# Attention in a hybrid encoder: the product with the values moves behind the transposes of the next unit, into the free columns of one of its PSUM banks

## The chip, the cores and the metric

One core of a Trainium2 chip runs the whole kernel as one program. The metric is the device time of that program in microseconds, as the median of several executions; less is better. One execution was also recorded by the hardware profiler, and all rows below come from that one.

## What is computed

The reference is an encoder of two layers. Each layer normalizes its input, multiplies it by one wide projection, and runs three token mixers beside each other: windowed attention, an mLSTM and a Mamba-2 SSD. Their outputs go through output projections, are gated, summed and projected once more. Two sequences (256 and 512 tokens, together six tiles of 128) share the weights. Only attention is touched. Cut to that part (`...` marks what is left out):

```python
def window_attention(q, k, v, sink):
    ...
    s = jnp.einsum('bnqhgd,bnkhd->bnhgqk', qb, kw).astype(jnp.float32) * (ATT_HEAD_DIM ** -0.5)
    ...
    mx = jnp.maximum(jnp.max(s, axis=-1, keepdims=True), sk)
    p = jnp.exp(s - mx)
    p = p / (jnp.sum(p, axis=-1, keepdims=True) + jnp.exp(sk - mx))
    o = jnp.einsum('bnhgqk,bnkhd->bnqhgd', p.astype(v.dtype), vw)
    return o.reshape(bsz, s_len, ATT_HEADS * ATT_HEAD_DIM)
...
    ya = window_attention(aq, ak, av, attn_sink) * jax.nn.silu(az)
```

There are 8 query heads of width 64 and 2 heads of keys and values. A tile of 128 queries sees its own tile of keys and its neighbours in the same sequence, so two or three tiles.

## The kernel before

**The stream of large matmuls.** The program walks through a list of items (`ORDER`), each a projection from the normalized tokens or an output projection. A float32 number is split into a high and a low part of type float32r, and a product is three matmuls of such parts. These matmuls, 512 or 256 columns wide, are most of TensorE's work. `mm_c` and `mm_t` issue them and call `tick()` after every few.

**The mixers as filling.** The mixers are Python generators. `tick()` lets them issue as many steps as a planner (`Clock`) holds ready: it adds up a cost for every instruction on every engine, and a step may go when its inputs and its PSUM banks are free by the planner's time, which is that of TensorE (`now`). A generator says what it waits for: `yield` (its last step is done), `yield 1`, `yield 2` or `yield "pair"` (so many of the four PSUM banks 4 to 7, which `grab` gives out and `give` takes back), or a tuple (a flag that another step sets with `flag`). The order in which instructions are issued is so fixed when the program is built; on the chip semaphores, put in by the framework, hold an instruction until what it needs is there. The engines work through their queues in order.

**Attention.** `mix_att(l, g)` handles one group of four query heads in one layer. Its work is twelve units, one for each tile of queries and pair of heads, numbered here 0 to 11; a `Flow` keeps up to four of them in progress, each at least one step behind the one ahead. There are two layers and two groups, so four times twelve units, 48 in all. A unit's steps are:

1. Scores: two banks, one for each head; masked maximum on VectorE into the SBUF buffers `ps[0]` and `ps[1]`, 256 or 384 wide (`n`).
2. Exponentials with their sums on ScalarE, the reciprocal on VectorE, and the scaling by it on ScalarE (head 0) and GpSimd (head 1).
3. Transposes: two banks; TensorE transposes `ps[0]` into the first and `ps[1]` into the second, 128 columns at a time, and ScalarE copies each bank back into `ps[0]` and `ps[1]`.
4. Values: one more bank; TensorE multiplies the values by the transposed probabilities, head 0 into partitions 0 to 63 and head 1 into 64 to 127, 128 columns wide; VectorE multiplies the result by the gate.
5. ScalarE and GpSimd split that product into its high and low part.

In the profile the transposes of a unit are 4 MATMULs of 128 columns with two tiles of keys and 6 with three, one for each tile and head. The product with the values has 64 stationary columns (`128*64` in the rows); each of its float32 matmuls shows as two MATMULs, so it has 8 or 12.

**What hangs on attention.** In each layer the two groups run one after the other (`A0`, `A1`), then the four mLSTM heads, then the SSD. The item `oa0` in the large stream needs attention's output; `item_O` calls `finish_mixer((l, "A1"))` before it issues its first matmul, and this issues all that is left of attention at once.

The profile shows all instructions on line 332, which is the helper that records them for the planner; names (`psum<-F`, `psum<-H,R`) and shapes tell them apart. `H` holds the normalized tokens, `R` float32r data and split weights, `F` float32 data. MATMULs on `H,R` and `R,H`, and those on `R` 512 wide, are the large stream; those on `R` 256 or 384 wide in blocks of four are attention's scores.

Of the kernel before, what the change touches and what calls it, by code (L numbers as in the profile page):

```python
# [12 lines left out]
ALU = mybir.AluOpType  # L13
# [18 lines left out]
NT = 6  # L32
# [385 lines left out]
class Body:  # L418
# [1163 lines left out]
    def mix_att(self, l, g):  # L1582
        s, nc, F = self.S[l], self.nc, self.F
        v, sc = nc.vector, nc.scalar
        cb = s["cb"]
        yield Room(self.R, 4 * TOK)
        s["ya", g] = self.R.alloc(4 * TOK)
        if g == 0:
            yield Room(F, *[384] * 8, *[128] * 4, *[12] * 4)
            s["pr"] = Ring(F, 8, 384)  # L1590
            s["ar"] = Ring(F, 4, 128)
            s["as"] = Ring(F, 4, 12)
        q4 = s["q", g].ap.rearrange("p (h t) -> p h t", h=4)
        k4 = s["k"].ap.rearrange("p (x v t) -> p x v t", x=2, v=2)
        vv = s["v"].ap.rearrange("p (i c) -> p i c", i=NT)

        def unit(i, hp):
            seq = SEQ_TILES[0] if i < 2 else SEQ_TILES[1]
            ks = [j for j in (i - 1, i, i + 1) if j in seq]
            n = 128 * len(ks)  # L1600
            m0 = K_ATT + 128 * (ks[0] - i + 1)
            h0 = 4 * g + 2 * hp
            ts = slice(128 * i, 128 * i + 128)
            bs = yield 2
            sm = s["as"].next()
            ps = [s["pr"].next()[:, 0:n] for _ in range(2)]
            for e, b in enumerate(bs):
                for x in range(2):
                    nc.tensor.matmul(out=b[:, 0:n], lhsT=q4[:, 2 * hp + e, ts],
                                     rhs=k4[:, x, g, 128 * ks[0]:128 * ks[0] + n], start=x == 0, stop=x == 1)  # L1610
            for e, b in enumerate(bs):
                v.tensor_tensor_reduce(out=ps[e], in0=b[:, 0:n], in1=self.K[:, m0:m0 + n], scale=1.0, scalar=-3.0e38,
                                       op0=ALU.add, op1=ALU.max, accum_out=sm[:, e:e + 1])
            self.give(*bs)
            r, sink = s["qn"].ap[:, 8 * i + h0:8 * i + h0 + 2], cb[:, CB_SINK + h0:CB_SINK + h0 + 2]
            v.tensor_tensor(out=sm[:, 0:2], in0=sm[:, 0:2], in1=r, op=ALU.mult)
            v.scalar_tensor_tensor(out=sm[:, 2:4], in0=sm[:, 0:2], scalar=-1.0, in1=sink, op0=ALU.mult, op1=ALU.min)
            v.tensor_tensor(out=sm[:, 6:8], in0=sm[:, 2:4], in1=sink, op=ALU.subtract)
            yield
            for e in range(2):  # L1620
                sc.activation(out=ps[e], in_=ps[e], func=AF.Exp, bias=sm[:, 2 + e:3 + e], scale=r[:, e:e + 1],
                              accum_out=sm[:, 4 + e:5 + e])
            sc.activation(out=sm[:, 6:8], in_=sm[:, 6:8], func=AF.Exp)
            yield
            v.tensor_tensor(out=sm[:, 8:10], in0=sm[:, 4:6], in1=sm[:, 6:8], op=ALU.add)
            v.reciprocal(out=sm[:, 10:12], in_=sm[:, 8:10])
            yield
            sc.activation(out=ps[0], in_=ps[0], func=AF.Copy, scale=sm[:, 10:11])
            nc.gpsimd.tensor_scalar(out=ps[1], in0=ps[1], scalar1=sm[:, 11:12], scalar2=None, op0=ALU.mult)
            bs = yield 2  # L1630
            for e, b in enumerate(bs):
                for j in range(len(ks)):
                    self.transpose_to(b[:, 128 * j:128 * j + 128], ps[e][:, 128 * j:128 * j + 128])
            for e, b in enumerate(bs):
                sc.copy(ps[e], b[:, 0:n])
            self.give(*bs)
            b, = yield 1
            for j, kt in enumerate(ks):
                for e in range(2):
                    nc.tensor.matmul(out=b[64 * e:64 * e + 64, 0:128], lhsT=vv[:, kt, 64 * g:64 * g + 64],  # L1640
                                     rhs=ps[e][:, 128 * j:128 * j + 128], start=j == 0, stop=j == len(ks) - 1)
            o = s["ar"].next()
            v.scalar_tensor_tensor(out=o, in0=b[:, 0:128], scalar=0.5, in1=s["az", 2 * g + hp].ap[:, ts], op0=ALU.mult, op1=ALU.mult)
            self.give(b)
            yield
            y4 = s["ya", g].ap.rearrange("p (x j t) -> p x j t", x=2, j=2)
            hi, lo = (y4[:, x, hp, ts] for x in range(2))
            sc.copy(hi, o)
            yield
            nc.gpsimd.tensor_tensor(out=lo, in0=o, in1=hi.bitcast(F32), op=ALU.subtract)  # L1650

        yield Flow([unit(i, hp) for i in range(NT) for hp in range(2)], 4)
        s.pop(("q", g)).free()
        for j in (2 * g, 2 * g + 1):
            s.pop(("az", j)).free()
        if g == 1:
            for k in ("pr", "ar", "as", "k", "v", "qn"):
                s.pop(k).free()
# [336 lines left out]
```

## Time and profile before

| what | value |
|---|---|
| median of the runs timed | 1682.69 us (3 runs, 1682.54 to 1683.93) |
| the profiled execution | 1680.04 us |
| its span, first to last instruction | 1678.2 us |
| TensorE busy in the span | 1666.3 us, 99% |
| VectorE, ScalarE, GpSimd busy | 53%, 38%, 17% |
| granted clock of TensorE | 1.00 |

The profiled execution is 1.84 us longer than its span, which is what lies around the span. It is 2.65 us shorter than the median of the timed runs. A busy share of TensorE says that some matmul was in its pipeline; how densely the matmuls follow each other is read from their start times.

### The profile page before, as it was taken

How to read it: one execution, taken by the hardware profiler on the slowest of the kernel's cores; microseconds unless marked ns; L12 is line 12 of the kernel's file. 1: busy time of each engine (PE TensorE's matmuls, PEld its weight loads, DVE VectorE, ACT ScalarE, POOL GpSimd, SP SyncE). 2: the span in 40 equal slices, each digit the busy share in tenths (PEclk: the TensorE clock that was granted, in tenths of full speed). 3: DMA queues.
4: the chain of work that ended last, by engine and by line, in shares of the span. 5: the costliest groups of instructions: out<-in, count | busy, mean ns of one | idle time of the engine just before them, and what ended most of it. 6: DMA issues, size and time to landing. Idle time of an engine off the chain costs nothing. (4 is left out here: it accounts for less than half of the span.)

```text
span 1678.2 us, 25327 instructions
## 1 busy us (share of the span) xinstructions
PE 1666.3 (99%) x9898; PEld 1433.0 (85%) x9898; DVE 890.6 (53%) x2114; ACT 633.6 (38%) x1365; POOL 284.9 (17%) x398
## 2 busy tenths in 40 slices
PE   8999999999999999999999999999999999999999
PEld 6888888988887888888878878898888888888887
DVE  6663537644486962246347535465455869523541
ACT  5456653422333522233233646532332345132320
POOL 5513220000002020013034223100000020201220
PEclk9999999999999999999999999999999999999999
DMA  5110122222124633145202101222221146331522
GB/s 192 64 40 27 56 81 92 69 70 68 63 63 124 166 87 107 62 155 170 88 32 72 45 26 63 82 83 79 70 73 60 63 126 173 79 110 44 176 88 76
DMA packets 45434, 145.36 MB, mean 87 GB/s; under 512 B 5345, under 2 KB 6273, under 8 KB 45314
## 3 DMA queue, kind: packets, MB, share of 16 engines
q1 hardware_dynamic: 43010, 137.44, 24.6%
q0 software_dynamic: 2304, 6.29, 2.4%
q8 instruction: 78, 1.28, 0.3%
q14 instruction: 42, 0.34, 0.1%
HBM read 124.69 MB, written 19.02 MB: 86 GB/s over the span
## 5 line engine op out<-in xcount | busy, mean ns | idle before, releaser
L332 PE MATMUL psum<-H,R 128*128 128x512 f32 x4800 | 885.9, 340 | 0.0
L332 PEld LDWEIGHTS psum<-H,R 128*128 128x128 f32 x4800 | 734.1, 188 | 103.3 <-issue 5.1
L332 PE MATMUL psum<-R,H 128*128 128x512 f32 (+2 forms) x1752 | 386.5, 376 | 3.1 <-DVE H L332 1.6
L332 PEld LDWEIGHTS psum<-R,H 128*128 128x128 f32 x1752 | 305.0, 188 | 59.2 <-DVE H L332 2.5
L332 DVE TENSOR_TENSOR R<-F,R 128x1024 fp32r<-128x1024 f32 (+3 forms) x178 | 222.1, 1258 | 246.1 <-ACT R L332 244.5
L332 ACT ACTIVATE F<-F 128x128 f32<-128x128 f32 (+8 forms) x432 | 210.6, 517 | 184.6 <-DVE F L332 177.5
L332 DVE SCALAR_TENSOR_TENSOR F<-F 128x128 f32<-128x128 f32 (+5 forms) x644 | 236.4, 412 | 57.1 <-POOL F L332 31.3
L332 PE MATMUL psum<-F 128*128 128x128 f32 (+6 forms) x2002 | 251.4, 288 | 5.5 <-DMA F<-ng_dram 2.7
L332 PE MATMUL psum<-R 128*128 128x512 f32 (+2 forms) x1344 | 249.8, 336 | 0.0
L332 PEld LDWEIGHTS psum<-F 128*128 128x128 f32 (+3 forms) x2002 | 203.2, 162 | 48.0 <-issue 20.4
L332 ACT CAST R<-F 128x1024 fp32r<-128x1024 f32 (+3 forms) x226 | 194.6, 875 | 120.4 <-PE psum L332 52.4
L332 PEld LDWEIGHTS psum<-R 128*128 128x128 f32 x1344 | 203.9, 188 | 31.3 <-issue 4.6
L332 ACT ACTIVATE F<-psum 128x768 f32<-128x768 f32 (+2 forms) x124 | 89.2, 719 | 324.0 <-PE psum L332 313.4
L332 POOL TENSOR_TENSOR F<-F 128x512 f32<-128x512 f32 (+9 forms) x200 | 166.2, 841 | 253.3 <-ACT F L332 119.6
L332 POOL TENSOR_SCALAR F<-F 128x256 f32<-128x256 f32 (+9 forms) x114 | 81.5, 718 | 742.8 <-ACT F L332 524.2
L332 ACT COPY F<-psum 128x256 f32<-128x256 f32 (+6 forms) x262 | 95.5, 399 | 200.3 <-PE psum L332 193.1
L332 DVE SCALAR_TENSOR_TENSOR F<-F,psum 128x768 f32<-128x768 f32 (+3 forms) x124 | 88.5, 725 | 95.6 <-PE psum L332 53.0
L332 DVE SCALAR_TENSOR_TENSOR F<-psum,F 128x128 f32<-128x128 f32 (+4 forms) x75 | 37.5, 505 | 186.8 <-PE psum L332 182.8
L332 DVE TENSOR_TENSOR F<-F 128x2 f32<-128x2 f32 (+7 forms) x292 | 74.7, 266 | 26.0 <-ACT F L332 18.6
L332 DVE TENSOR_SCALAR F<-F 128x128 f32<-128x128 f32 (+3 forms) x206 | 59.4, 327 | 42.1 <-ACT F L332 22.2
L332 DVE TENSOR_TENSOR F<-F,psum 128x129 f32<-128x129 f32 (+2 forms) x104 | 35.8, 377 | 37.9 <-ACT F L332 23.0
L332 DVE CUSTOM_DVE_ANT_0 F<-psum,F 128x256 f32<-128x256 f32 (+1 forms) x96 | 40.9, 464 | 13.4 <-PE psum L332 13.1
(25 smaller groups left out, 277.1 us busy)
## 6 DMA issues: line engine op xcount, KB each, us to landing
F<-wts_dram SPq DMA_DIRECT2D x164, 512.0 KB, 3.6
F<-csd SPq DMA_DIRECT2D x32, 384.0 KB, 6.1
F<-x_dram SPq DMA_DIRECT2D x12, 512.0 KB, 6.2
F<-md SPq DMA_DIRECT2D x16, 384.0 KB, 5.6
mg<-F SPq DMA_DIRECT2D x16, 384.0 KB, 2.6
mg<-F POOLq DMA_DIRECT2D x16, 384.0 KB, 4.8
F<-mg SPq DMA_DIRECT2D x16, 384.0 KB, 4.2
x<-F SPq DMA_DIRECT2D x6, 512.0 KB, 2.6
```

Of the source, the lines that this page charges most:

```text
L332: r = fn(*args, **kw)
```

## The change

A unit no longer takes a bank of its own for the product with the values. After its transposes it leaves a function (`values`) in a list. The next unit of the same group, right after it has issued its own transposes and their two copies, calls that function with columns 384 to 511 of its first bank, which transposes use at most up to column 383. So the product of unit `num - 1` is issued behind the transposes of unit `num`, in the same step. Two flags order the steps: `"pr"` says that a unit's transposed probabilities are there, and the next unit issues no transposes before it; `"pv"` says that a unit's product has been issued, and its last two steps wait for it. The last unit of a group still takes a bank of its own.

```diff
+            o = s["ar"].next()
+
+            def values(b):
+                for j, kt in enumerate(ks):
+                    for e in range(2):
+                        nc.tensor.matmul(out=b[64 * e:64 * e + 64, :], lhsT=vv[:, kt, 64 * g:64 * g + 64],
+                                         rhs=ps[e][:, 128 * j:128 * j + 128], start=j == 0, stop=j == len(ks) - 1)
+                v.scalar_tensor_tensor(out=o, in0=b, scalar=0.5, in1=s["az", 2 * g + hp].ap[:, ts], op0=ALU.mult, op1=ALU.mult)
+
+            yield (l, "pr", g, num - 1) if num else None
             bs = yield 2
             for e, b in enumerate(bs):
                 for j in range(len(ks)):
                     self.transpose_to(b[:, 128 * j:128 * j + 128], ps[e][:, 128 * j:128 * j + 128])
             for e, b in enumerate(bs):
                 sc.copy(ps[e], b[:, 0:n])
+            self.flag(l, "pr", g, num)
+            if left:
+                left.pop()(bs[0][:, 384:512])
+                self.flag(l, "pv", g, num - 1)
             self.give(*bs)
-            b, = yield 1
-            for j, kt in enumerate(ks):
-                for e in range(2):
-                    nc.tensor.matmul(out=b[64 * e:64 * e + 64, 0:128], lhsT=vv[:, kt, 64 * g:64 * g + 64],
-                                     rhs=ps[e][:, 128 * j:128 * j + 128], start=j == 0, stop=j == len(ks) - 1)
-            o = s["ar"].next()
-            v.scalar_tensor_tensor(out=o, in0=b[:, 0:128], scalar=0.5, in1=s["az", 2 * g + hp].ap[:, ts], op0=ALU.mult, op1=ALU.mult)
-            self.give(b)
-            yield
+            if num < last:
+                left.append(values)
+                yield (l, "pv", g, num)
+            else:
+                b, = yield 1
+                values(b[:, 0:128])
+                self.give(b)
+                yield
```

Here `num = 2 * i + hp`, `last = 11`, and `left` is one list for the twelve units of a group.

## Rows read from the trace of the kernel before

**Rows 1.** The page: span, busy time and share of each engine.
```profile
span 1678.2 us, 25327 instructions
PE 1666.3 (99%) x9898; PEld 1433.0 (85%) x9898; DVE 890.6 (53%) x2114; ACT 633.6 (38%) x1365; POOL 284.9 (17%) x398
```

**Rows 2.** Waits of TensorE over the span: total us, times, longest; two largest of six.
```profile
PE psum L332 <- DMA F<-ng_dram: 2.7, 1, 2.7
PE psum L332 <- DVE H L332: 1.6, 2, 1.2
```

**Rows 3.** One stretch of attention: us, busy time by engine, PEclk, DMA share, GB/s.
```profile
113.00:184.00 71.00, 71.00 (x466) 57.69 (x465) 29.00 (x132) 44.80 (x138) 22.53 (x31) 1.00 0.07 23
```

**Rows 4.** Timeline of TensorE: start, us from start to last end, operation.
```profile
166.08 0.60 PE L332 MATMUL psum<-F 128*128 128x128 f32 x4
166.43 1.64 PE L332 MATMUL psum<-R,H 128*128 128x512 f32 x6
168.00 0.66 PE L332 MATMUL psum<-F 128*64 128x128 f32 x8
168.59 3.02 PE L332 MATMUL psum<-R,H 128*128 128x512 f32 x12
...
174.26 1.55 PE L332 MATMUL psum<-R,H 128*128 128x512 f32 x6
175.65 0.64 PE L332 MATMUL psum<-R 128*128 128x256 f32 x4
...
179.44 1.25 PE L332 MATMUL psum<-F 128*64 128x128 f32 x12
180.44 1.64 PE L332 MATMUL psum<-R,H 128*128 128x512 f32 x6
...
182.60 1.66 PE L332 MATMUL psum<-R,H 128*128 128x512 f32 x6
184.10 0.60 PE L332 MATMUL psum<-F 128*128 128x128 f32 x4
```

**Rows 5.** Timeline of all engines, 238.9 to 241.6 us (idle time before in brackets).
```profile
238.96 1.19 PE L332 MATMUL psum<-F 128*128 128x128 f32 x12
239.44 0.65 ACT L332 COPY F<-psum 128x256 f32<-128x256 f32 x2 [0.49 <-PE psum L332]
239.49 0.42 PEld L332 LDWEIGHTS psum<-F 128*64 128x64 f32 x8 [0.17 <-issue]
240.08 0.97 PE L332 MATMUL psum<-H,R 128*128 128x512 f32 x4
...
240.98 0.66 PE L332 MATMUL psum<-F 128*64 128x128 f32 x8
...
241.57 0.96 PE L332 MATMUL psum<-H,R 128*128 128x512 f32 x4
```

**Rows 6.** Timeline of TensorE and ScalarE, a unit with three tiles of keys.
```profile
151.49 0.82 PE L332 MATMUL psum<-F 128*128 128x128 f32 x6
...
152.07 0.86 ACT L332 COPY F<-psum 128x384 f32<-128x384 f32 x2 [1.02 <-PE psum L332]
```

**Rows 7.** Groups by shape, ScalarE, 113 to 242 us: busy us, mean ns.
```profile
L332 ACT COPY F<-psum 128x256 f32<-128x256 f32 x44 | 14.2, 376 | 18.8 <-PE psum L332 18.6
L332 ACT COPY F<-psum 128x384 f32<-128x384 f32 x16 | 6.9, 483 | 13.5 <-PE psum L332 11.3 <-issue 2.2
```

**Rows 8.** The chain that ended last, in order of time: start, us, what.
```profile
978.79 0.04 issue
978.84 460.68 PE psum L332 x2887
```

**Rows 9.** Groups by shape, TensorE, 241.6 to 249.95 us, then 1073.4 to 1084.05 us.
```profile
L332 PE MATMUL psum<-H,R 128*128 128x512 f32 x24 | 8.5, 398 | 0.0
...
L332 PE MATMUL psum<-H,R 128*128 128x512 f32 x24 | 8.8, 406 | 0.0
```

**Rows 10.** Timeline of TensorE behind the last product of attention, second layer.
```profile
1069.08 6.16 PE L332 MATMUL psum<-H,R 128*128 128x512 f32 x34
```

More of the change, by code (lines that the diff above doesn't have):

```diff
@@ L1595, in mix_att @@
         vv = s["v"].ap.rearrange("p (i c) -> p i c", i=NT)
+        left = []
+        last = 2 * NT - 1
         def unit(i, hp):
+            num = 2 * i + hp
             seq = SEQ_TILES[0] if i < 2 else SEQ_TILES[1]
```

## The prediction

> **What bounds the kernel now.** I read the page first: TensorE is busy in 1666.3 of 1678.2 us and no other engine is above 53% [rows 1]. The view of waits then says how little TensorE stands still: six rows, 8.2 us in all, 2.7 of it the first load and the rest mostly between the layers [rows 2]. In attention's stretch it never stands still, and its clock is 1.00, the 2.4 GHz level [rows 3]. So the end is set by what TensorE issues, one instruction behind the other, and whatever holds it back holds back the large stream queued behind. Work taken from ScalarE, VectorE or the banks is worth nothing unless it shortens TensorE's queue. A busy share of 99% hides losses between matmuls, so everything below is read from starts in the timeline.
>
> **What an insertion costs today.** In the rows, T is a unit's block of transposes, V its product with the values. Six matmuls of the stream alone take 1.39 us (174.26 to 175.65). Between a T and a V they take 1.57 (166.43 to 168.00), so leaving a T and entering a V cost 0.18 together; behind a V and ahead of a T they take 1.50 (182.60 to 184.10), so leaving a V costs 0.11 [rows 4]. T itself lasts 0.35 to the next start with four transposes (166.08 to 166.43), V 0.59 with eight matmuls (168.00 to 168.59) [rows 4]. A T and a V apart therefore cost 0.35 + 0.59 + 0.18 + 0.11 = 1.23 us.
>
> **What the move saves.** The change joins T of unit n with V of unit n-1, T first, 11 times in each of four runs of attention, 44 times. The trace has this order once already, on separate banks: T at 238.96, the first weights of V at 239.49, the stream again at 240.08 [rows 5]. That is 1.12 us, and 0.11 for leaving V makes 1.23: the same as apart. T takes 0.53 ahead of a V where it takes 0.35 ahead of the stream, so the cost of turning from 128 to 64 stationary columns is paid either way. The other order, V first and T behind it, is cheaper: 1.00 for the two (179.44 to 180.44), plus the 0.18, is 1.18 [rows 4]. Going through the list of blocks, I counted this order at 21 of the 48 products of before, seven with matmuls 512 wide alone in front and fourteen with pairs of 512 and 256. After the change a T that directly follows a V is unlikely, since it must wait for the copies of the T before. So the move loses 21 x 0.05 = 1.05 us and saves nothing. No instruction is added or removed on TensorE, and no DMA is touched; ScalarE, VectorE and GpSimd do what they did.
>
> **What the move adds.** Both blocks now use one bank. ScalarE's copy of `bs[0]` is issued before V and reads that bank; V writes other columns of it. I take it that the framework orders accesses to PSUM bank by bank, so that the first weight load of V waits for this copy (not for the copy of `bs[1]`, which is another bank). No row of before has such a pair, since every product had a bank of its own; the kernel's own code points the same way, for the last columns of the last tile take a fresh pair of banks (`if c0 == 768: p = self.gbank()[:, 256:512]`) where the bank just being read had room. From below the price is nothing, if columns are told apart. From above it is the time until the second copy ends. Between them I take the first copy, as the code issues it.
>
> The price with two tiles of keys: T starts at 238.96, ScalarE begins the first copy at 239.44 [rows 5], a copy takes 0.376 [rows 7], so it ends at 239.82; TensorE starts 0.05 after the instruction that it waited for (978.79 to 978.84) [rows 8], so at 239.87. Without the wait it started at 239.49: a stall of 0.38. With three tiles: the copy begins at 152.07, 0.58 after T [rows 6], takes 0.483 [rows 7], and with the 0.05 V may start 1.11 after T. Without the wait it would be 0.53 plus two more transposes, (0.82 - 0.60) / 2 = 0.11 each [rows 4, 6], so 0.75: a stall of 0.36. The turn from 128 to 64 columns lies inside both and isn't added. ScalarE was not late for any of the 48 pairs: in the instruction list the first copy begins about 0.09 after its transposes each time, so no queue lengthens the wait.
>
> Seven of the units 1 to 11 have two tiles of keys and four have three, so 28 stalls of 0.38 and 16 of 0.36: 10.6 + 5.8 = 16.4 us. Behind each on TensorE stands only the large stream, and nothing covers it there. Against the profiled execution: 1680.04 + 16.4 + 1.05 = 1697.5 us. The median of the timed runs is 2.65 us above that execution; the same 17.4 on 1682.69 gives 1700.1, and I forecast 1700.
>
> The Trainium skill, "PSUM — Partial Sum Buffer", section "PSUM bank collisions raise a hardware error", says that two engines may not touch the same bank in the same 32 partitions at once, whatever the columns, that the chip does not hold one back, and that programs must order such accesses by bank. By that rule the sum is the one above, plus 17.4 us; if columns were enough, plus 1 us. No row of before shows a case of it.
>
> **Steps that ScalarE and the planner move.** V of unit n now waits in the order for T of unit n+1, and a unit keeps its place among the four in progress for longer, so attention may end later in the order. In the second layer the first matmul of `oa0` comes after 1073.3, 4 us behind the last product [rows 9, 10]. In the first layer it comes at 241.57, directly behind V of unit 11 at 240.98 [rows 5]: the 48 matmuls of its gate fill 241.6 to 249.95, 24 of each width [rows 9]. So a delay in the order there turns into time in which only attention's chain is issued. The units still follow T by T, and T never waited for V before, so I take nothing for it. The upper bound is a few units left over: each needs T, the first copies and V in a row with no stream between, some 0.53 + 0.38 + 0.59 = 1.5 us, or about 3 with the scaling in front, so 3 to 12 us for one to four units.
>
> **Rivals.**
> 1. *Attention ends late.* Same stalls, and two or more units left at `oa0` in the first layer, and one in the second: 17.4 + 9 = +26, 1709. For it: the 241.57 above. Against: the order of T blocks hardly changes. 0.13.
> 2. *V waits for both copies.* The pair of copies lasts 0.65 and 0.86 [rows 5, 6] where the first takes 0.376 and 0.483, so 28 x 0.27 + 16 x 0.38 = 13.6 more: 1714. Against: `bs[1]` is another bank. 0.05.
> 3. *No wait at all.* The change then does nothing on TensorE but lose the 21 cheap orders: 1683.7, no change that counts. 0.08.
> 4. *Faster.* No wait, and a V directly behind a T costs as little as a T behind a V: each of 44 then saves 0.05 in itself and the 0.09 that is half of the 0.18 in front of V: 6.2 - 1.05 = 5.1, so 1677.6. It decides if T with V behind it lasts under about 0.40 us rather than the 0.53 of the one row [rows 5]. 0.04.
>
> **How the numbers follow.** The forecast has 0.70. Its own range is 1694 to 1705: stalls of 0.25 to 0.45, or one unit late. Rival 1 reaches 1711, and leaving out rivals 2, 3 and 4 leaves 0.17 outside, so the range is 1692 to 1711. A change under 0.2% (3.4 us) can't be told from none. Slower is the forecast and rivals 1 and 2, 0.88; same is rival 3, 0.08; faster rival 4, 0.04.
>
> **What would show it.** In the waits, TensorE idles before `psum<-F` 128*64 groups, ended by ScalarE writing F, some 44 times. That view counts only the time in which no matmul is in the pipeline, so it will show less than 16.4, perhaps 0.1 to 0.2 each. In the timeline, T to V takes 0.91 and 1.11 instead of 0.53 and 0.75. Scores, transposes and copies last what they did, and the span outside attention stays. The prediction is wrong if V starts before the copy of its bank ends, if ScalarE's copies come later than before, or if `oa0` follows a stretch with no stream.

## The result and the profile after

The changed kernel takes 1705.63 us (median of 4 runs, 1705.51 to 1708.32) against 1683.31 for the kernel before on the same chip; the ratio is 1.0141, 95% interval 1.0128 to 1.0153. The forecast was 1700.0, from 1692 to 1711. The profiled execution is 1705.60 us, its span 1703.8. The profiled execution of before lay 3 us under the median of its runs, so the two spans differ by 25.6 us where the medians differ by 22.3.

The page of the changed kernel, span and busy time ([rows 1] before; PE and PEld are TensorE's matmuls and weight loads, DVE is VectorE, ACT is ScalarE, POOL is GpSimd). Every engine issues as many instructions as before, and TensorE's share falls.

```profile
span 1703.8 us, 25307 instructions
PE 1671.8 (98%) x9898; PEld 1436.2 (84%) x9898; DVE 891.6 (52%) x2114; ACT 636.3 (37%) x1365; POOL 281.3 (17%) x398
```

TensorE's waits in the changed kernel: who was waited for, us in all, times, longest.

```profile
PE psum L332 <- ACT F L332: 17.9, 44, 1.2
PE psum L332 <- DMA F<-ng_dram: 2.7, 1, 2.7
PE psum L332 <- DVE F L332: 2.6, 4, 1.1
PE psum L332 <- DVE R L332: 2.3, 3, 1.2
PE psum L332 <- DVE H L332: 1.6, 2, 1.3
PE psum L332 <- POOL F L332: 1.0, 1, 1.0
PE psum L332 <- ACT H L332: 0.4, 2, 0.3
```

The first row is new and has 44 entries, one for each product that moved. The others add up to 10.6 us, against 8.2 in all before.

Timeline of the changed kernel at a unit with two tiles of keys; the idle time in front of a row stands in brackets.

```profile
118.94 0.60 PE L332 MATMUL psum<-F 128*128 128x128 f32 x4
...
119.41 0.65 ACT L332 COPY F<-psum 128x256 f32<-128x256 f32 x2 [0.51 <-PE psum L332]
119.84 0.42 PEld L332 LDWEIGHTS psum<-F 128*64 128x64 f32 x8 [0.54 <-ACT F L332]
119.84 0.66 PE L332 MATMUL psum<-F 128*64 128x128 f32 x8 [0.30 <-ACT F L332]
...
120.43 0.50 PE L332 MATMUL psum<-H,R 128*128 128x512 f32 x1
```

And at one with three tiles of keys:

```profile
151.53 0.82 PE L332 MATMUL psum<-F 128*128 128x128 f32 x6
152.11 0.86 ACT L332 COPY F<-psum 128x384 f32<-128x384 f32 x2 [1.41 <-PE psum L332]
152.64 0.64 PEld L332 LDWEIGHTS psum<-F 128*64 128x64 f32 x12 [0.53 <-ACT F L332]
```

From the transposes T to the product V it is now 0.90 us and 1.11. The forecast had 0.91 and 1.11; the one T with V behind it in the kernel before took 0.53 [rows 5]. In these two units ScalarE's copies begin as early after T as they did (0.47 and 0.58); V's first weights are loaded 0.05 after the first copy ends, and in the meantime the whole large stream stands behind them.

### The profile page after: what moved, and what is told of

Read it like the earlier page. It is cut to its first block, busy times and chain, and to the rows that moved or that the text cites. A ratio compares the mean times of both kernels' runs of the same rounds, so it can differ in the third digit from the quotient of the medians.

```text
span 1703.8 us, 25307 instructions
## 1 busy us (share of the span) xinstructions
PE 1671.8 (98%) x9898; PEld 1436.2 (84%) x9898; DVE 891.6 (52%) x2114; ACT 636.3 (37%) x1365; POOL 281.3 (17%) x398
## 4 chain that ended last, share of the span: by engine, by line
PE 93%; ACT 2%; DVE 2%; issue 1%; DMA 1%; POOL 0%; SPq 0%; ACTq 0%; DVEq 0%; POOLq 0%
PE psum L332 93%; ACT F L332 2%; DVE R L332 1%; DVE F L332 1%; ACT R L332 0%; DMA F<-wts_dram 0%; DMA F<-cstb_dram 0%; POOL F L332 0%; ACT H L332 0%; DVE H L332 0%; DMA F<-ng_dram 0%; SPq L332 0%; ACTq L332 0%; DVEq L332 0%; POOLq L332 0%
## 5 line engine op out<-in xcount | busy, mean ns | idle before, releaser
L332 PE MATMUL psum<-F 128*128 128x128 f32 (+6 forms) x2002 | 251.9, 287 | 24.5 <-ACT F L332 17.9
L332 POOL TENSOR_SCALAR F<-F 128x256 f32<-128x256 f32 (+9 forms) x114 | 74.2, 653 | 780.7 <-ACT F L332 563.0
```

What stands on the lines that cost most here:

```text
L332: r = fn(*args, **kw)
```

## Two theories and the experiments

**The wait**: nearly all of the loss is TensorE standing in front of V until ScalarE has copied the bank that V writes. **The order** (the rival): the loss comes from V standing behind the next unit's transposes, which lengthens attention's chain and costs changes between 128 and 64 stationary columns, whichever bank it uses. Each kernel is set against the kernel before on its own chip (1681.14 us beside the first four, 1682.36 beside the others).

**e1: the same step, a bank of its own.**

```diff
-            bs = yield 2
+            bs = yield 3 if num else 2
+            own, bs = bs[2:], bs[:2]
...
-                left.pop()(bs[0][:, 384:512])
+                left.pop()(own[0][:, 0:128])
...
-            self.give(*bs)
+            self.give(*bs, *own)
```

> The product with the values stays in the same step behind the next unit's transposes, with the same flags, but goes into a third bank that the unit asks for together with its two. Theory (the wait): what the change costs is TensorE waiting for ScalarE's copy out of the bank that the product writes; with another bank the wait is gone, T to V is 0.53 us with four transposes and 0.75 with six (0.90 and 1.11 in the changed kernel), TensorE's waits ended by ScalarE on psum<-F all but vanish, and the time is 1684 to 1688: the kernel before plus 1 us for the lost order V ahead of T and up to 4 us of other waits that the new order moves. Rival (the order): the time is lost because each product now stands behind the next unit's transposes and attention's chain is longer; the bank changes nothing, 1700 to 1706.

Measured: 1684.11 us, ratio 1.0017 (1.0008 to 1.0027). Its waits on ScalarE's F tiles, and its timeline at one pair of T and V:

```profile
PE psum L332 <- ACT F L332: 0.4, 1, 0.4
...
117.44 1.19 PE L332 MATMUL psum<-F 128*128 128x128 f32 x12
117.96 0.42 PEld L332 LDWEIGHTS psum<-F 128*64 128x64 f32 x8 [0.16 <-issue]
118.40 0.66 ACT L332 COPY F<-psum 128x256 f32<-128x256 f32 x2
```

V starts 0.53 after T though ScalarE's copies have not even begun (118.40). Over all 44, T to V is 0.53 and 0.75. The flags are those of the changed kernel, and V still stands right behind T 44 times; but asking for three banks moves the units to other places in the stream (the last V of the first layer comes behind 444 of its matmuls on `H,R`, in the changed kernel behind 412). Some 19 of 22 us are gone, so the order as the main cause falls.

**e2: the second bank instead of the first.**

```diff
-                left.pop()(bs[0][:, 384:512])
+                left.pop()(bs[1][:, 384:512])
```

> The changed kernel with the product in the free columns of the second bank instead of the first. Theory (the wait, bank by bank): the product now waits for the second copy, which ends 0.27 us later with 256 columns and 0.38 later with 384; T to V becomes 1.17 and 1.49, and the time rises by 28 x 0.27 + 16 x 0.38 = 13.6 us to about 1719. Rival (the order), and a rule by which the product waits for both copies anyway: nothing changes, 1704 to 1708.

Measured: 1721.71 us, ratio 1.0244 (1.0228 to 1.0259). Its waits and timeline:

```profile
PE psum L332 <- ACT F L332: 32.3, 45, 1.5
...
118.90 0.60 PE L332 MATMUL psum<-F 128*128 128x128 f32 x4
...
119.38 0.65 ACT L332 COPY F<-psum 128x256 f32<-128x256 f32 x2 [0.79 <-PE psum L332]
...
120.08 0.42 PEld L332 LDWEIGHTS psum<-F 128*64 128x64 f32 x8 [0.81 <-ACT F L332]
```

The pair of copies ends at 120.03 and V is loaded 0.05 later. T to V is 1.17 and 1.49 where ScalarE is in time, as expected, and where ScalarE begins late (in eight units of the changed kernel, see below) V is later still. TensorE's matmuls come in the same order here as in the changed kernel, one by one, so only the bank differs. So V waits for the copy of its own bank and no other, though it writes columns that no copy reads. The Trainium skill asks for such an order in "PSUM — Partial Sum Buffer", section "PSUM bank collisions raise a hardware error" (accesses are to be ordered by bank, whatever the columns); e1 and e2 agree with it, by 0.37 us a unit for the first bank and 0.64 to 0.75 for the second. What would happen without the wait was not tried. The time is 2.7 us above the 1719 expected: T to V accounts for 0.6 of that and TensorE's other waits for 0.7, and the rest stays open.

**e3: the same bank, V ahead of the copies.**

```diff
-            for e, b in enumerate(bs):
-                sc.copy(ps[e], b[:, 0:n])
-            self.flag(l, "pr", g, num)
             if left:
                 left.pop()(bs[0][:, 384:512])
                 self.flag(l, "pv", g, num - 1)
+            for e, b in enumerate(bs):
+                sc.copy(ps[e], b[:, 0:n])
+            self.flag(l, "pr", g, num)
```

> The changed kernel with the product issued ahead of the two copies rather than behind them, into the same columns of the same bank. Theory (the wait): the bank is the same, but now the copies stand behind the product in the order, so ScalarE waits for TensorE and not the other way round; T to V 0.53 and 0.75, the copies begin about 0.9 to 1.1 us later, nothing on TensorE waits for them, 1684 to 1688. Rival (the order): still each product behind the next transposes, and attention's chain longer by the later copies: 1704 or more.

Measured: 1691.18 us, ratio 1.0060 (1.0045 to 1.0075). TensorE no longer waits between T and V (0.53 and 0.75), which the wait theory said; but the time is 3 us above its range. Its waits, ScalarE and VectorE behind one V, and TensorE before another unit's transposes:

```profile
PE psum L332 <- ACT F L332: 5.3, 8, 0.9
...
114.64 1.19 PE L332 MATMUL psum<-F 128*128 128x128 f32 x12
...
115.87 0.29 DVE L332 SCALAR_TENSOR_TENSOR F<-psum,F 128x128 f32<-128x128 f32 x1 [2.18 <-PE psum L332]
...
116.25 0.65 ACT L332 COPY F<-psum 128x256 f32<-128x256 f32 x2 [0.29 <-DVE F L332]
...
129.96 1.25 PE L332 MATMUL psum<-F 128*128 128x128 f32 x12 [0.89 <-ACT F L332]
```

Now the copies wait for V and, the bank being the same, for VectorE's gate product too: they begin 1.61 after T (114.64 to 116.25) instead of 0.47. ScalarE falls behind, and eight other blocks of TensorE wait for it. The bank's price is paid by another engine, and part of it comes back to TensorE.

**e4: a step between the copies and V.**

```diff
             self.flag(l, "pr", g, num)
+            yield
             if left:
                 left.pop()(bs[0][:, 384:512])
```

> The changed kernel with one step between the copies and the product: the product comes in a later turn of the planner, still into the free columns of the first bank, which the unit keeps until then. Theory (the wait): the large stream now stands between transposes and product and covers the copies; TensorE's waits ended by ScalarE are gone and the time is 1683 to 1687, or a few us more if the banks that are kept longer delay attention. Rival (the order): 1700 to 1706, since the product still comes after the next unit's transposes.

Measured: 1687.39 us, ratio 1.0035 (1.0022 to 1.0047), at the upper edge of what was expected. TensorE's waits:

```profile
PE psum L332 <- DVE F L332: 3.2, 5, 1.2
PE psum L332 <- DVE R L332: 2.8, 3, 1.2
...
PE psum L332 <- ACT F L332: 1.7, 3, 1.1
```

The bank is the same, and the stream now covers the copies. ScalarE's three waits are the three places where V still stood right behind T. So the wait costs because nothing stands between T and V. What is left are waits for VectorE elsewhere, below.

**e5: V ahead of the transposes, in the same step.** `values` returns VectorE's gate product as a function, issued behind the copies.

```diff
             bs = yield 2
+            gate = left.pop()(bs[0][:, 384:512]) if left else None
             for e, b in enumerate(bs):
...
                 sc.copy(ps[e], b[:, 0:n])
             self.flag(l, "pr", g, num)
-            if left:
-                left.pop()(bs[0][:, 384:512])
+            if gate:
+                gate()
```

> The changed kernel with the product of the unit before issued ahead of the unit's own transposes, in the same step and the same bank; the copies follow, and VectorE's gate product behind them. Theory (the wait): nothing on TensorE stands behind a copy of its own bank any more, and a product with transposes directly behind it takes 1.18 us for both rather than 1.23, now 44 times rather than 21: 1.2 us less than before on that account, some 3 us more for waits that the new order moves, so 0 to 3 us above the kernel before. Rival: moving two blocks into one bank costs even without TensorE waiting, since gate product and copies now take turns on the bank and attention runs later, as when the product stood ahead of the copies: 8 to 12 us above.

Measured: 1682.33 us, ratio 1.0004 (0.9995 to 1.0013). Timeline:

```profile
115.44 1.25 PE L332 MATMUL psum<-F 128*64 128x128 f32 x12
...
116.44 1.63 PE L332 MATMUL psum<-H,R 128*128 128x512 f32 x8
116.57 0.64 ACT L332 COPY F<-psum 128x256 f32<-128x256 f32 x2
116.97 0.29 DVE L332 SCALAR_TENSOR_TENSOR F<-psum,F 128x128 f32<-128x128 f32 x1 [2.58 <-ACT F L332]
```

V and T together take 1.00 with two tiles of keys (115.44 to 116.44), and this order now comes 44 times. The bank's order is V, T, copy, gate product, and only VectorE waits, which is busy for about half of the span [rows 1]. So the bank can be shared at no price; it is the place of V behind the copies that costs. This is as fast as the kernel before, not faster: the order saves 0.05 us 23 times more often, and TensorE's other waits grow by as much (1.1 us).

**e6: the first bank's copy on VectorE.**

```diff
             for e, b in enumerate(bs):
-                sc.copy(ps[e], b[:, 0:n])
+                if e:
+                    sc.copy(ps[e], b[:, 0:n])
+                else:
+                    v.tensor_copy(ps[e], b[:, 0:n])
```

> The changed kernel with the copy of the first bank on VectorE, the second still on ScalarE. In the changed kernel the copy begins late in 8 of 44 units, because ScalarE still has exponentials of another unit queued, and this is 4.8 of the 21 us between T and V. Theory: with VectorE, which reads 128 columns of PSUM in 0.29 us and 256 in 0.42, T to V stays near 0.9 and 1.1, the late ones go or become others where VectorE is behind with splitting weights; 0 to 5 us less than the changed kernel. Rival: the late ones are not ScalarE's queue but come from the transposes themselves being late, and stay: same as the changed kernel within 1 us, with the same eight units late.

Measured: 1703.81 us, ratio 1.0129 (1.0115 to 1.0143), 2.6 us under e7. Timeline at one unit, and VectorE's copies from 113 to 242 us (mean ns behind the comma):

```profile
117.73 0.60 PE L332 MATMUL psum<-F 128*128 128x128 f32 x4
...
118.14 0.42 DVE L332 COPY F<-psum 128x256 f32<-128x256 f32 x1 [0.26 <-PE psum L332]
...
118.62 0.42 PEld L332 LDWEIGHTS psum<-F 128*64 128x64 f32 x8 [0.53 <-DVE F L332]
...
L332 DVE COPY F<-psum 128x256 f32<-128x256 f32 x16 | 6.8, 425 | 15.7 <-PE psum L332 14.9 <-ACT R L332 0.8
L332 DVE COPY F<-psum 128x384 f32<-128x384 f32 x8 | 4.5, 558 | 11.2 <-PE psum L332 11.2
```

TensorE waits for VectorE in ScalarE's place. The copy is slower there (0.425 and 0.558 against 0.376 and 0.483 [rows 7]), so most units take 0.97 and 1.14 to 1.21; but none takes longer than that, where the changed kernel has eight. So the late eight came from ScalarE, as far as a kernel whose units also fall elsewhere in the stream can show it.

**e7: the changed kernel on the second chip.**

> The changed kernel again, unaltered, to stand beside the others on one chip: 22 to 25 us above the kernel before.

Measured: 1706.38 us, ratio 1.0146 (1.0133 to 1.0160), 24 us above, with the same eight late units.

**e8: the kernel before with the flag `pr` alone.**

```diff
+            num = 2 * i + hp
+            yield (l, "pr", g, num - 1) if num else None
             bs = yield 2
...
                 sc.copy(ps[e], b[:, 0:n])
+            self.flag(l, "pr", g, num)
             self.give(*bs)
```

> The kernel before with one part of the change: a unit issues its transposes only when the copies of the unit before have been made (the flag pr); the product keeps its own bank and its own step. Theory: the flag alone hardly binds, 0 to 1 us above the kernel before, with TensorE's waits in all near 8 us. Rival: the 3 us that are left with a bank of its own come from this flag, which moves attention against the weights: 2 to 4 us above.

Measured: 1684.16 us, ratio 1.0011 (1.0002 to 1.0020), waits of TensorE 9.0 us in all. Its ten runs lie between 1681.4 and 1687.9, so between the two expectations nothing is settled beyond that the flag costs at most 0.2%.

**All of them in one sum.** For each kernel: how much T to V grew beyond 0.53 and 0.75, summed over its instruction list; 0.05 us for every V with a T directly behind it that the kernel lacks against the 21 of before (a minus sign where it has more); and TensorE's other waits less the 8.2 us of before. The last columns are the sum and the measured difference of the medians.

| kernel | T to V | order | other waits | sum | measured |
|---|---|---|---|---|---|
| changed (e7) | 21.0 | 1.05 | 2.0 | 24.0 | 24.0 |
| e1 own bank | 0 | 1.05 | 2.8 | 3.9 | 3.0 |
| e2 second bank | 35.2 | 1.05 | 2.7 | 38.9 | 40.6 |
| e3 V ahead of copies | 0.4 | 1.05 | 7.5 | 9.0 | 10.0 |
| e4 step apart | 2.0 | 0.4 | 3.7 | 6.1 | 6.3 |
| e5 V first | 0 | -1.15 | 1.1 | 0 | 0 |
| e6 copy on VectorE | 18.9 | 1.05 | 1.7 | 21.6 | 21.5 |
| e8 flag alone | 0.4 | -0.05 | 0.5 | 0.9 | 1.8 |

## Why the prediction was right, and where it was short

**The stall.** Right in place, cause and price: 44 waits, for the first copy, ended by ScalarE. With ScalarE in time T to V is 0.90 and 1.11, so the stall is 0.37 and 0.36 and 16 us in all, where 0.38 and 0.36 and 16.4 were forecast.

**"So no queue lengthens the wait": the term that was short.** In eight units ScalarE began the copy 0.13 to 0.78 us late, or 0.90 where it had two copies of other work to make first, and T to V took up to 1.8. That adds 4.8 us, which the sum had at nothing. The changed kernel at unit 1 of the first group:

```profile
115.20 0.60 PE L332 MATMUL psum<-F 128*128 128x128 f32 x4
...
115.35 0.59 ACT L332 ACTIVATE F<-F 128x256 f32<-128x256 f32 x1
...
115.93 0.59 ACT L332 ACTIVATE F<-F 128x2 f32<-128x2 f32 x2
116.42 0.63 ACT L332 COPY F<-psum 128x256 f32<-128x256 f32 x2
116.83 0.42 PEld L332 LDWEIGHTS psum<-F 128*64 128x64 f32 x8 [1.27 <-ACT F L332]
```

and the same place in the kernel before:

```profile
114.95 1.25 PE L332 MATMUL psum<-F 128*64 128x128 f32 x12
...
115.59 0.59 ACT L332 ACTIVATE F<-F 128x2 f32<-128x2 f32 x2
116.09 0.64 ACT L332 COPY F<-psum 128x256 f32<-128x256 f32 x2
```

Before, V (0.59 us) stood ahead of these transposes, inside the block that begins at 114.95, and ScalarE got through another unit's exponentials meanwhile; its copy came only 0.01 us later than usual. The change took V out of that place, the transposes came some 0.7 earlier against ScalarE's queue (0.73 ahead of the exponential at 115.93, where before it was 0.05 ahead of the one at 115.59), and the wait ran into the exponentials. I had read "never late" off an order that the change removes. That the lateness comes from ScalarE is what e6 says, and in seven of the eight units the timeline too, since ScalarE worked without a break up to the copy; that V had covered it is read from these two timelines alone. In the eighth unit ScalarE had been idle for 1.40 us and still began 0.28 late, and the profile does not show why:

```profile
991.95 0.82 PE L332 MATMUL psum<-F 128*128 128x128 f32 x6
...
992.81 0.86 ACT L332 COPY F<-psum 128x384 f32<-128x384 f32 x2 [1.40 <-PE psum L332]
```

The reading of the kernel before was also not quite right. One of its 48 first copies was late, 0.42 after its transposes instead of about 0.09:

```profile
1056.50 0.82 PE L332 MATMUL psum<-F 128*128 128x128 f32 x6
...
1057.41 0.83 ACT L332 COPY F<-psum 128x384 f32<-128x384 f32 x2
```

And six of the 48, this one among them, have no idle time of ScalarE in front of the copy, so there was no slack to lose. Three of the six belong to unit 1 of a group, and in the changed kernel unit 1 is late in all four groups, which is 3.1 of the 4.8 us.

**What the move saves.** Nothing, as forecast; 0.53 and 0.75 came out in e1 for 44 pairs, and the cheap order's 1.00 us (two tiles of keys) in e5.

**What was taken at nothing.** TensorE's other waits grew by 2.0 to 2.4 us, on VectorE. These two waits of the kernel before became 2.6 and 2.3 us:

```profile
PE psum L332 <- DVE F L332: 1.5, 4, 0.7
PE psum L332 <- DVE R L332: 0.9, 2, 0.5
```

At one place of the changed kernel TensorE waits for the low part of a weight, which is queued on VectorE behind a gate product, which itself comes behind the stalled V:

```profile
153.67 0.29 DVE L332 SCALAR_TENSOR_TENSOR F<-psum,F 128x128 f32<-128x128 f32 x1 [2.70 <-PE psum L332]
153.88 1.22 DVE L332 TENSOR_TENSOR R<-F,R 128x1024 fp32r<-128x1024 f32 x1
...
155.14 0.50 PE L332 MATMUL psum<-R,H 128*128 128x512 f32 x1 [1.19 <-DVE R L332]
```

Such waits differ from kernel to kernel without a pattern that I could name (2.8 more in e1, 3.7 in e4, 1.1 in e5); what in the planner's order sets them stays open.

**The range.** The forecast was 17.4 us more; 22.3 were measured, and 24.0 in e7. The two terms for which the sum had nothing, 4.8 and 2.0 to 2.4 us, are as large as the excess of e7 and some 2 us larger than the first one. The forecast's own range ended at 1705, and 1705.63 lies inside 1692 to 1711 only by the room that was made for rival 1, which did not come. To that extent the hit is luck. One of the prediction's own signs of being wrong, copies of ScalarE that come later than before, came true in the eight units.

**The rivals.** Attention did not end late. It ended earlier in the order: in the first layer the last V is again at 240.98, but with 412 of the stream's matmuls on `H,R` issued instead of 480, and the stream goes on for 68 more before `oa0`. V waiting for both copies, and no wait at all, are excluded by T to V; the faster rival by the 0.53. "In the waits less than 16.4, perhaps 0.1 to 0.2 each" was wrong: the view shows 0.30 of the 0.37, since a stall of 0.37 outlasts the matmuls in the pipeline by more than I took, and with the late units the row adds up to 17.9.

## What to carry to other kernels

Ask of every instruction moved into a buffer that another engine is reading who must now wait for whom, and at what grain the program orders them: here whole PSUM banks, so free columns were no free room. On the engine that bounds the kernel a wait of 0.4 us needs other work in front of it; the same sharing costs nothing when the block is issued ahead of the writes that the other engine waits for (e5). An engine that is "never late" in a profile is so in that order of instructions, and a change that takes work out from in front of its customer must be priced with its queue.

## What the runs showed that I had not expected

VectorE's copy of 256 fp32 columns out of PSUM took 0.425 us and ScalarE's 0.376; for 384 columns 0.558 and 0.483. So VectorE was the slower engine for this copy, and swapping engines gained only by the queue.

The terms read from the trace add up to the measured difference within 2 us for all eight kernels of the table (for the changed kernel's first measurement they give some 24 against 22.3), though spans and medians of one kernel lie up to 3 us apart: the sum was better compared with medians on one chip than with the difference of two spans.
